# A hybrid attention, recurrence and mixture-of-experts layer: rows of most experts summed during the last five blocks, a written order of experts, and the shared expert's first products moved forward

## The chip, the cores and the metric

The kernel runs on one core of a Trainium2 chip. The metric is the device time of one execution in microseconds (us). Engines: PE (TensorE) multiplies matrices, DVE (VectorE), ACT (ScalarE) and POOL (GpSimd) work element by element, SP issues most DMAs. Each engine runs its own queue in order; semaphores join them.

## The reference

One layer over 512 latent tokens and 256 context tokens, width 1024, all float32. The first half (modulated norm, latent attention, a recurrent block, an output projection added to `x`) is not touched in what it computes. The second half is a mixture of 64 experts and one shared expert, each token using the 8 experts with the best scores:

```python
def swiglu(u, w_gate, w_up, w_down):
    return (jax.nn.silu(u @ w_gate) * (u @ w_up)) @ w_down

def moe_ffn(h, ...):                       # h: 512 x 1024
    scores = jax.nn.sigmoid(h @ router_w)  # 64 experts, groups of 8
    ...                                    # 4 best groups, then 8 best experts
    w = ROUTED_SCALE * w / w.sum(-1, keepdims=True)
    routed = routed_experts(h, eidx, w, exp_w_gate, exp_w_up, exp_w_down)
    return routed + swiglu(h, sh_w_gate, sh_w_up, sh_w_down)
```

Gate and up weights of an expert are 1024 x 256 each, its down weight 256 x 1024: 3 MiB an expert, 192 MiB for all. The result is gated, added to the residual, and normalised once more.

## The kernel before

**Stages.** By the trace's time: the modulation, input projection, recurrence and attention (to about 333 us), the output projection and the second norm (to about 390), the router and the shared expert (to 439), the 64 experts (439 to 1043), the final sum and norm (to 1113).

**Blocks of experts.** The router ranks the experts by load. Rank r has room for `caps[r]` rows, a multiple of 32; the rooms, laid end to end in the order `order`, are cut into 46 blocks of up to 128 rows. `n` is a place in that order, and a block holds rows of one to four experts. For a block, POOL gathers the tokens' rows from `h2d` (`stage_gather`, three blocks ahead), PE transposes them (`stage_trans`), multiplies by the gate and up weights (`stage_gu`, tile `gu`), transposes the product (`stage_at`) and multiplies by the down weight (`stage_down`, tile `dn`). DVE scales the result into `y`, and POOL scatters its rows to `yd` in DRAM, where each token has eight rows, one for each of its choices. PE's instructions stand in the order in which the program writes them (`manual_schedule`); the other compute engines are ordered by a scheduler with priorities.

**Weights.** There are six places for gate and up weights (tags `g0` to `g5`) and six for down weights (`d0` to `d5`). Expert `n` uses the places of `n % 6`, so its load waits until expert `n - 6` has been used for the last time. SP issues the loads in order, 1 MiB each, with at most three outstanding (`wload`). Three experts of fixed number come first; the others wait for the router's `eids`.

**The shared expert.** `sgu(t)` makes gate and up products of 128 tokens (tile `psg`), `smul` their product, `sdn` the down product and the sum with the residual `x1`, stored to `acc` in DRAM. They stand between the router's steps. The shared weights and `x1` lie in places of the experts' weights (`g4`, `d4`, `g2`).

**The end.** After the last block SP loads `acc` into `xs`. A loop over overfull experts follows (`n_ov` runs, none with these inputs), and all engines meet at it. Then SP loads the 16 MiB of `yd` in 16 pieces (`yload`, tiles `yl`), PE sums four of the eight rows of each token (`fsum`, tile `fs`), DVE adds the others, and for each 128 tokens a norm (`fsq`, `frs`) and a scaling (`fout`) lead to the store of the output.

Of the kernel before, what the change touches and what calls it, by code (L numbers as in the profile page):

```python
# [8 lines left out]
F32 = mybir.dt.float32  # L9
# [68 lines left out]
NTAIL = 8  # L78
OUTST = 3
LEAD = 22  # L80
# [20 lines left out]
def tile_kernel(tc, x, c, ctx, c_ctx, w_mod, b_mod, norm_mix_g, w_in, q_norm_g, w_q_up, kv_norm_g, w_kv_up,  # L101
# [13 lines left out]
    acc = dram.tile([S, D], F32, name="acc")  # L115
# [820 lines left out]
    x1 = pW1.tile([P, NT, D], F32, tag="g2", name="x1")  # L936
# [24 lines left out]
    wgu_s = pW1.tile([P, 2, KT, FF], F32, tag="g4", name="wgu_s")  # L961
# [21 lines left out]
    POOL.tensor_scalar(isf, ir[:, 0:E], float(NF), None, op0=OP.is_ge)  # L983
    icf = pR.tile([P, 1], F32, name="icf")
# [74 lines left out]
    @prio("sgu")  # L1059
    def sgu(t):  # L1060
        p = sgp[t] = psx("psg")
        for k in range(KT):
            PE.matmul(p, h2T[:, k, t * P:(t + 1) * P], wgu_s[:, :, k, :], start=(k == 0), stop=(k == KT - 1))
        sga[t] = et("act", "sg")
        ACT.activation(sga[t], p[:, 0:FF], AF.Silu)
# [5 lines left out]
    @prio("sdn")  # L1071
    def sdn(t):
# [3 lines left out]
        sgT = et("aT", "sgT").rearrange("p (k t) -> p k t", k=2)  # L1076
        cp("sgT", "A", sgT, pt[:, 0:FF].rearrange("p (k t) -> p k t", k=2))
        p = pw("psd")
        for n in range(2):
            for k in range(2):  # L1080
                PE.matmul(p[:, n * 512:(n + 1) * 512], sgT[:, k, :], wd_s[:, k, n * 512:(n + 1) * 512],
                          start=(k == 0), stop=(k == 1))
        tb = et("y", "tb")
        DVE.tensor_tensor(tb, p, g2b, op=OP.mult)  # L1084
        DVE.tensor_tensor(tb, tb, x1[:, t], op=OP.add)
        ACT.dma_start(acc[t * P:(t + 1) * P, :], tb)
# [38 lines left out]
    for n, r in enumerate(order):  # L1125
        for u in range(0, caps[r], 32):
            if at % P == 0:
                b = Blk()
                b.q, b.units, b.dyn = len(blocks), [], None
                blocks.append(b)  # L1130
            blocks[-1].units.append((n, r, u))
            at += 32
    for b in blocks:
        ns = [u[0] for u in b.units]
        w = 128 if len(set(ns)) == 1 else 64 if len(ns) == 4 and ns[0] == ns[1] and ns[2] == ns[3] else 32
        b.tiles = [(c, min(w, 32 * len(ns) - c)) + b.units[c // 32] for c in range(0, 32 * len(ns), w)]
        b.rows = 32 * len(ns)

        b.runs = []
        for c, (n, r, u) in enumerate(b.units):  # L1140
            if b.runs and b.runs[-1][2] == n:
                b.runs[-1][1] += 32
            else:
                b.runs.append([32 * c, 32, n, r, u])
    loads, seen, last = [], set(), {}
    for b in blocks:
        new = [n for n in dict.fromkeys(u[0] for u in b.units) if n not in seen]
        seen.update(new)
        loads += [(n, "g") for n in new] + [(n, "d") for n in new]
        for u in b.units:  # L1150
            last[u[0]] = b.q
# [3 lines left out]
    def load_upto(m):  # L1155

        while loads:
            n, what = loads[0]
            r = order[n]
            if n > m or r < E - NF and "routed" not in state or n >= NW and last[n - NW] > state["done"]:  # L1160
                return
            loads.pop(0)
            if n not in eid:
                eid[n] = r - (E - NF) if r >= E - NF else SP.value_load(eids[0:1, r:r + 1], min_val=0, max_val=E - 1)
            if what == "g":
                wg[n] = load_gu(eid[n], GS[n % NW])
            else:
                wd_[n] = load_d(eid[n], n % NW)
# [13 lines left out]
    logits(2)  # L1182
    sgu(0)
# [87 lines left out]

    for src in (pm1, ws):
# [3 lines left out]
        sT = et("sv", "sT")  # L1276
        cp("sT", "A", sT[0:E, :], p[0:E, :])
# [34 lines left out]
    def stage_gather(b, p=None):  # L1312
# [15 lines left out]
        DVE.scalar_tensor_tensor(t2[0:m], tk[0:m], float(TOPK), p[0:m, 3:4], op0=OP.mult, op1=OP.add)  # L1328
        DVE.tensor_scalar(b.iy[0:m], t2[0:m], float(FAR * TOPK), None, op0=OP.add)
# [7 lines left out]
    smul(1)  # L1337
    stage_sel(blocks[0])
    stage_sel(blocks[1])
    sdn(0)  # L1340
    sgu(2)
    stage_gather(blocks[0], pn("ix0"))
    smul(2)
    sdn(1)
    stage_gather(blocks[1], pn("ix1"))
    stage_sel(blocks[2])
    sgu(3)
    load_upto(NW - 2)
# [10 lines left out]
    st_E2 = ExitStack()  # L1359
    pE2 = st_E2.enter_context(tc.tile_pool(name="pE2", bufs=1))  # L1360
# [36 lines left out]
    def stage_down(b):  # L1397
# [8 lines left out]
        DVE.scalar_tensor_tensor(y[0:m], p[0:m], b.w[0:m], g2b[0:m], op0=OP.mult, op1=OP.mult)  # L1406
        ins = POOL.indirect_dma_start(out=yd, out_offset=bass.IndirectOffsetOnAxis(ap=b.iy[0:m, :1], axis=0),  # L1407
                                      in_=y[0:m], in_offset=None, bounds_check=S * TOPK - 1, oob_is_err=False).ins
        if b.dyn is None:
            if yw:  # L1410
                tc.declare_no_dep(ins, group="yd", reason="every token and choice has a row of its own")
            tc.add_to_no_dep_group("yd", ins)
            yw.append(ins)
# [48 lines left out]
    st_M = ExitStack()  # L1462
    st_M.enter_context(tc.manual_schedule(engines={mybir.EngineType.PE}))
# [3 lines left out]
    for i, b in enumerate(blocks):  # L1467
# [10 lines left out]
        load_upto(E - 1)  # L1478
        if i in (10, 12, 14, 16):
            got = next(table)  # L1480
            nov, ovr, obase = got or (None,) * 3
    st_M.close()

    xs = pW1.tile([P, NT, D], F32, tag=f"g{GS[(E - 6) % NW]}", name="xs")
    for t in range(NT):
        SP.dma_start(xs[:, t], acc[t * P:(t + 1) * P, :])
# [3 lines left out]
    with tc.For_i(0, n_ov, 1) as iv:  # L1490
# [3 lines left out]
        b.rows, b.q, b.tiles, b.runs = P, 0, [(0, P, -1, 0, 0)], [(0, P, -1, 0, 0)]  # L1494
# [18 lines left out]
    st_F = ExitStack()  # L1513
    psf = st_F.enter_context(tc.tile_pool(name="psf", bufs=1, space=PSUM))

# [7 lines left out]
    ydv = yd.rearrange("(t p k) f -> t p k f", p=P, k=TOPK)  # L1523
    yl = {}

    place = [GS[n % NW] for n in range(E - 5, E)]
    small = [n % NW for n in range(E - 6, E)]

    def yload(t, k0, n, buf):
        kind, i = buf  # L1530
        if kind == "g":
            z = (pW0 if i < 2 else pW1 if i < 5 else pW2).tile([P, 4, D], F32, tag=f"g{i}", name="yl")
        else:
            z = (pE2 if i == 5 else pW1).tile([P, 2, D], F32, tag=f"d{i}", name="yl")
        for k in range(0, n, 2):
            ins = SP.dma_start(z[:, k:k + 2, :], ydv[t, :, k0 + k:k0 + k + 2, :]).ins  # L1536
            for w in yw:
                after(ins, w, "rows of all experts")
            for j in range(2):
                yl[t, k0 + k + j] = z[:, k + j, :]  # L1540


    @prio("fsum")
    def fsum(t):
        p = psf.tile([P, D], F32, tag="fs", name="fs", bufs=2)
        for n0 in range(0, D, 512):
            for k in range(4):
                PE.matmul(p[:, n0:n0 + 512], ident, yl[t, k][:, n0:n0 + 512], start=(k == 0), stop=(k == 3))  # L1548
        for k in range(4, TOPK):
            DVE.tensor_tensor(xs[:, t], xs[:, t], yl[t, k], op=OP.add)  # L1550
        DVE.tensor_tensor(xs[:, t], xs[:, t], p, op=OP.add)  # L1551
# [26 lines left out]
    for t in range(NT):  # L1578
        if t < 2:
            yload(t, 0, 4, ("g", place[2 * t]))  # L1580
            yload(t, 4, 4, ("g", place[2 * t + 1]))
        elif t == 2:
            yload(t, 0, 4, ("g", place[4]))
            yload(t, 4, 2, ("d", small[0]))
            yload(t, 6, 2, ("d", small[1]))
        else:
            for k in range(0, TOPK, 2):
                yload(t, k, 2, ("d", small[2 + k // 2]))
    for t in range(NT):
        fsum(t)  # L1590
        fsq(t)
        frs(t)
        fout(t)
    st_F.close()
# [32 lines left out]
```

## Time and profile before

| | us |
|---|---|
| median of 3 runs | 1115.37 (1114.18 to 1116.23) |
| the profiled execution | 1114.81 |
| its span, first to last instruction | 1112.8 |
| outside the span | 2.0 |
| PE busy | 996.2 (90% of the span) |
| DVE, ACT, POOL busy | 484.3, 255.7, 223.4 |

The span is what the rows below are measured in: a time in them is counted from the span's start. A busy PE does not say that PE works at its peak, and its clock has two levels: PEclk is the share that was granted. An engine's row names the line of the kernel, the operation, what it writes and reads, and in brackets the idle time before it with what ended it. A DMA row (SPq) is the issue, not the transfer.

### The profile page before, as it was taken

Reading aid. Unit: us, or ns where it says so; the run is one execution under the profiler, and the core shown is the slowest. Engines: PE = TensorE matmul, PEld = TensorE weight load, DVE = VectorE, ACT = ScalarE, POOL = GpSimd, SP = SyncE. Lnnn points to the kernel's source line nnn. Section 1 sums busy time; section 2 is a strip of 40 time slices with the busy share of each in tenths; the row PEclk is TensorE's granted clock in tenths of the full one; section 3 lists DMA queues with packets and bytes.
Section 4 is the critical chain, followed back from the end, with each engine's and each line's share of the span. In section 5 each row is a group of like instructions: output and inputs, shape, how many; then the busy total and the mean of one; then the engine's idle time right before and its main releaser. Section 6 shows DMA issues by size and latency. Waiting matters only on the chain. (4 is left out here: it accounts for less than half of the span.)

```text
span 1112.8 us, 17435 instructions
## 1 busy us (share of the span) xinstructions
PE 996.2 (90%) x6813; PEld 515.6 (46%) x6813; DVE 484.3 (44%) x1064; ACT 255.7 (23%) x468; POOL 223.4 (20%) x219
## 2 busy tenths in 40 slices
PE   3899989799989998999999999999999999995482
PEld 2687654567779853443443344333333333331131
DVE  5527594988765865223222232222322223220065
ACT  3433545756661210011000110000100001000011
POOL 3382341346100001111111111111111111110001
PEclk9899999889999999999999999999999999997797
DMA  9834644200009543999999898989879999989694
GB/s 294 266 96 154 206 161 133 77 1 1 1 2 365 226 195 132 416 394 417 419 409 360 333 390 346 395 323 399 339 289 401 399 413 414 399 319 414 251 421 186
DMA packets 75404, 310.34 MB, mean 279 GB/s; under 512 B 12747, under 2 KB 31234, under 8 KB 48442
## 3 DMA queue, kind: packets, MB, share of 16 engines
q1 hardware_dynamic: 60412, 271.79, 63.2%
q0 software_dynamic: 13936, 34.26, 8.1%
q10 hardware_dynamic: 974, 3.17, 0.8%
q8 instruction: 54, 0.88, 0.3%
q14 instruction: 28, 0.23, 0.1%
HBM read 293.31 MB, written 30.29 MB: 291 GB/s over the span
## 5 line engine op out<-in xcount | busy, mean ns | idle before, releaser
L1382 PE MATMUL gu<-wgu,hT 128*32 128x512 f32 (+2 forms) x2160 | 333.0, 597 | 11.1 <-DMA wgu<-in_exp_w_up_dram 10.4
L1382 PEld LDWEIGHTS gu<-wgu,hT 128*32 128x32 f32 (+2 forms) x2160 | 105.4, 120 | 230.2 <-issue 225.9
L1403 PE MATMUL dn<-wd,aT 128*32 128x512 f32 (+2 forms) x1080 | 169.1, 596 | 16.6 <-ACT aT L124 15.4
L1385 DVE TENSOR_TENSOR act<-act,gu 128x256 f32<-128x256 f32 (+1 forms) x46 | 19.4, 421 | 297.8 <-ACT act L1384 297.8
L1384 ACT ACTIVATE act<-gu 128x256 f32<-128x256 f32 (+1 forms) x46 | 17.7, 385 | 511.7 <-PE gu L1382 511.7
L1332 POOL DMA_INDIRECT hg<-h2d,bix x46 | 47.6, 1034 | 425.9 <-issue 310.4
L1406 DVE SCALAR_TENSOR_TENSOR y<-dn,bw,g2b 128x1024 f32<-128x1024 f32 (+1 forms) x46 | 59.0, 1283 | 138.2 <-PE dn L1403 138.2
L1403 PEld LDWEIGHTS dn<-wd,aT 128*32 128x32 f32 (+2 forms) x1080 | 48.7, 119 | 100.8 <-issue 78.8
L1407 POOL DMA_INDIRECT yd<-y,biy x46 | 46.8, 1017 | 191.9 <-DVE y L1406 182.5
L1370 PEld LDWEIGHTS tr<-ident,hg 128*128 128x128 f32 (+1 forms) x368 | 39.9, 141 | 37.1 <-issue 34.1
L1370 PE MATMUL tr<-ident,hg 128*128 128x128 f32 (+1 forms) x368 | 49.7, 278 | 1.3 <-DVE tb L1084 1.3
L1548 PE MATMUL fs<-yl,ident 128*128 128x512 f32 x64 | 32.1, 654 | 20.3 <-DMA yl<-yd 18.1
L829 PE MATMUL pTr<-ident,P 128*128 128x128 f32 x192 | 30.7, 300 | 9.8 <-DVE P L820 7.7
L1306 DVE TENSOR_TENSOR sv<-iot,posR 128x256 bf16<-128x256 f32 (+3 forms) x93 | 37.1, 411 | 0.0
L812 DVE TENSOR_REDUCE nm<-pS 128x1 f32<-128x768 f32 x32 | 30.3, 951 | 11.2 <-PE pS L810 10.8
L124 ACT COPY PT<-pTr 128x384 f32<-128x384 f32 x64 | 28.0, 482 | 29.0 <-PE pTr L829 28.7
L124 ACT COPY hT<-tr 128x512 f32<-128x512 f32 (+1 forms) x46 | 26.9, 584 | 34.0 <-PE tr L1370 32.5
L840 PE MATMUL po<-PT,vsb 128*64 128x128 f32 x384 | 30.8, 299 | 1.7 <-ACT PT L124 1.7
L454 PE MATMUL pmx<-wm,csil 128*32 128x512 f32 x128 | 31.9, 606 | 0.0
L124 DVE COPY hT<-tr 128x512 f32<-128x512 f32 (+1 forms) x46 | 31.3, 680 | 0.0
L1548 PEld LDWEIGHTS fs<-yl,ident 128*128 128x128 f32 x64 | 12.7, 208 | 39.8 <-DMA yl<-yd 20.4
L829 PEld LDWEIGHTS pTr<-ident,P 128*128 128x128 f32 x192 | 24.1, 153 | 14.8 <-issue 7.7
(473 smaller groups left out, 1472.9 us busy)
## 6 DMA issues: line engine op xcount, KB each, us to landing
wgu<-in_exp_w_gate_dram SPq DMA_DIRECT2D x64, 1024.0 KB
wgu<-in_exp_w_up_dram SPq DMA_DIRECT2D x64, 1024.0 KB
wd<-in_exp_w_down_dram SPq DMA_DIRECT2D x64, 1024.0 KB
wm<-in_w_mod_dram SPq DMA_DIRECT2D x32, 512.0 KB
yl<-yd SPq DMA_DIRECT2D x16, 1024.0 KB
wm<-in_w_mod_dram SPq DMA_DIRECT2D x8, 1024.0 KB
win<-in_w_in_dram SPq DMA_DIRECT2D x5, 1024.0 KB
xz<-in_x_dram SPq DMA_DIRECT2D x4, 512.0 KB
```

The lines of the kernel that those rows point to most:

```text
L124: (e.copy if e is ACT else e.tensor_copy)(dst, src)
L454: PE.matmul(pm[32 * g:32 * g + 32, :], csil[:, kk, :], wmp[n, g // 2][:, (g % 2) * 512:(g % 2 + 1) * 512], start=(kk == 0), stop=(kk == KT ...
L829: PE.transpose(p[:, j * P:(j + 1) * P], Pm[u][:, k * P:(k + 1) * P], ident)
L840: PE.matmul(po[i][64 * hh:64 * hh + 64, t * P:(t + 1) * P], vsb[:, k, 2 * i + hh, :], PTt[i, t, hh][:, k, :], start=(k == 0), stop=(k == N ...
L1306: DVE.tensor_tensor(sv[:, :, c:c + w], iot[:, u:u + w][:, None, :].to_broadcast([P, NT, w]), col_[:, :, None].to_broadcast([P, NT, w]), op ...
L1332: POOL.indirect_dma_start(out=b.hg[0:m], out_offset=None, in_=h2d, in_offset=bass.IndirectOffsetOnAxis(ap=b.ix[0:m, :1], axis=0), bounds_c ...
L1370: PE.transpose(p[:, i * m:(i + 1) * m], b.hg[0:m, (i0 + i) * P:(i0 + i + 1) * P], ident[0:m, 0:m])
L1382: PE.matmul(p[c:c + w, :], b.hT[:, k, c:c + w], wg[n][:, :, k, :], start=(k == 0), stop=(k == KT - 1))
L1403: PE.matmul(p[c:c + w, n0:n0 + 512], b.aT[:, k, c:c + w], wd_[n][:, k, n0:n0 + 512], start=(k == 0), stop=(k == 1))
L1406: DVE.scalar_tensor_tensor(y[0:m], p[0:m], b.w[0:m], g2b[0:m], op0=OP.mult, op1=OP.mult)
L1407: ins = POOL.indirect_dma_start(out=yd, out_offset=bass.IndirectOffsetOnAxis(ap=b.iy[0:m, :1], axis=0), in_=y[0:m], in_offset=None, bounds ...
L1548: PE.matmul(p[:, n0:n0 + 512], ident, yl[t, k][:, n0:n0 + 512], start=(k == 0), stop=(k == 3))
```

## The change

In the diff's order. (1) The experts' order is written out. The last five ranks in it have room for at most 128 rows, and each starts a block of its own (`LATE = 5`); there are still 46 blocks. (2) The rows of these five blocks are no longer scattered to `yd`: POOL adds them by an accumulating DMA to `acc`, which has 128 rows more for empty places. (3) Since their rows of `yd` are not written now, `yd` is filled with zeros from `zt` during the attention: 16 MiB in four DMAs and 0.5 MiB for the new rows of `acc`. (4) `sgu` is written further forward, the third tile in three pieces between the router's steps; the down products are split in two halves on other PSUM tiles; the residual is kept in place (`x1`). `x1` and the shared gate and up weights change places (`g2`, `g4`), and `d4` and `d5` do. The places of `d5` are opened earlier, and so is the load of experts 3 and 4 (`load_upto(NW - 2)`). (5) `sum_loads` issues the 16 loads of `yd` after the blocks 40 to 45, each pair of rows to a place of weights that has been used for the last time. The sums in PE and DVE stand before the loop over overfull experts, the first adds before the last block. (6) DVE's order is the written one from the first block on. (7) At the end `acc` is loaded as `ya`, and one add for each 128 tokens joins it to the sum.

```diff
+ORDER = [61, 62, 63, 35, 60, 48, 52, 21, 43, 38, 9, 50, 34, 2, 46, 28,
...
+LATE = 5
+    acc = dram.tile([S + P, D], F32, name="acc")
+    zt = modrow.rearrange("p a b -> p (a b)")
+    POOL.memset(zt, 0.0)
+    SP.dma_start(acc[S:S + P, :], zt)
+    for t in range(NT):
+        SP.dma_start(yd.rearrange("(t p k) f -> t p k f", p=P, k=TOPK)[t], zt[:, None, :].to_broadcast([P, TOPK, D]))
...
-    x1 = pW1.tile([P, NT, D], F32, tag="g2", name="x1")
+    x1 = pW1.tile([P, NT, D], F32, tag="g4", name="x1")
-    wgu_s = pW1.tile([P, 2, KT, FF], F32, tag="g4", name="wgu_s")
+    wgu_s = pW1.tile([P, 2, KT, FF], F32, tag="g2", name="wgu_s")
...
+    def sdp(t):
+        tb = et("y", "tb")
+        x_ = x1[:, t]
+        for n0 in range(0, D, 512):
+            p = psx("psd")
             for k in range(2):
+                PE.matmul(p, sgT[t][:, k, :], wd_s[:, k, n0:n0 + 512], start=(k == 0), stop=(k == 1))
+            DVE.tensor_tensor(tb[:, n0:n0 + 512], p, g2b[:, n0:n0 + 512], op=OP.mult)
+        DVE.tensor_tensor(x_, tb, x_, op=OP.add)
+        ACT.dma_start(acc[t * P:(t + 1) * P, :], x_)
...
+    GS, DS, NW = (5, 0, 1, 2, 3, 4), (0, 1, 2, 3, 5, 4), 6
...
+        if n >= E - LATE:
+            at = 0
...
+        if b.late:
+            DVE.tensor_scalar(b.iy[0:m], tk[0:m], float(FAR), spad[0:m], op0=OP.add, op1=OP.min)
...
+        if b.late:
+            POOL.indirect_dma_start(out=acc, out_offset=bass.IndirectOffsetOnAxis(ap=b.iy[0:m, :1], axis=0),
+                                    in_=y[0:m], in_offset=None, bounds_check=S + P - 1, oob_is_err=True, compute_op=OP.add)
+            return
...
+    pairs = [(t, k) for t in range(NT) for k in range(0, TOPK, 2)]
+    homes = [("d", E - 6)] + [(w, n) for n in range(E - 5, E) for w in "dgh"]
+    def sum_loads(i):
...
+        while rest and last[rest[0][1][1]] <= i:
+            (t, k), (w, n) = rest.pop(0)
...
+            ins = SP.dma_start(z, ydv[t, :, k:k + 2, :]).ins
...
+        if not loads:
+            sum_loads(i)
+        if i == NB - 2:
+            for k in (0, 2, 4):
+                add_pair(0, k, k == 0)
...
+    add_pair(0, 6, False)
+    for t in range(1, NT):
...
+        for k in range(4):
+            for h in range(2):
+                PE.matmul(fs[h], ident, yl[t, k - k % 2][:, k % 2, h * 512:(h + 1) * 512], start=(k == 0), stop=(k == 3))
+        add_pair(t, 4, True)
+        add_pair(t, 6, False)
+        for h in range(2):
+            x_ = xs[:, t, h * 512:(h + 1) * 512]
+            DVE.tensor_tensor(x_, x_, fs[h], op=OP.add)
...
-    for t in range(NT):
-        SP.dma_start(xs[:, t], acc[t * P:(t + 1) * P, :])
...
+    for t in range(NT):
+        SP.dma_start(ya[:, t], acc[t * P:(t + 1) * P, :])
     def fsum(t):
...
+        DVE.tensor_tensor(xs[:, t], xs[:, t], ya[:, t], op=OP.add)
```

How it moves instructions at the end, on SP. Before, from the last expert's load to the loop over overfull experts (L1489 and L1490):

```order
L1104 ISA
L1104 DMA wd<-in_exp_w_down_dram 128x2048
L1486 DMA xs<-acc 128x1024 x4
L1489 TENSOR_LOAD nov
L1489 ISA x2
L1490 COMPARE_AND_BRANCH
L1490 UNCONDITIONAL_BRANCH x2
```

The 16 loads of `yd` (L1536) stand behind that loop there. Now, on SP, the same stretch (the loop is L1578 and L1579):

```order
L1119 ISA
L1119 DMA wd<-in_exp_w_down_dram 128x2048
L1523 DMA yl<-yd 128x2048 x16
L1578 TENSOR_LOAD nov
L1578 ISA x2
L1579 COMPARE_AND_BRANCH
L1579 UNCONDITIONAL_BRANCH x2
```

The 16 loads have moved ahead of the loop, and the load of `acc` behind it.

On PE, the last two blocks before (`gu` gate and up products, `tr` and `at` transposes, `dn` down products; 32 rows of an expert to a matmul):

```order
L1403 MATMUL dn<-wd,aT 32x512 x16
L1382 MATMUL gu<-wgu,hT 32x512 x32
L1370 MATMUL tr<-ident,hg 128x96 x8
L1393 MATMUL at<-ident,act 128x128 x2
L1403 MATMUL dn<-wd,aT 32x512 x16
L1382 MATMUL gu<-wgu,hT 32x512 x24
L1393 MATMUL at<-ident,act 128x96 x2
L1403 MATMUL dn<-wd,aT 32x512 x12
L1489 TENSOR_LOAD nov
```

These two blocks hold seven experts. PE's last two blocks now, and what follows them:

```order
L1438 MATMUL dn<-wd,aT 128x512 x4
L1417 MATMUL gu<-wgu,hT 128x512 x8
L1405 MATMUL tr<-ident,hg 128x128 x8
L1428 MATMUL at<-ident,act 128x128 x2
L1438 MATMUL dn<-wd,aT 128x512 x4
L1417 MATMUL gu<-wgu,hT 128x512 x8
L1428 MATMUL at<-ident,act 128x128 x2
L1438 MATMUL dn<-wd,aT 128x512 x4
L1569 MATMUL fs<-yl,ident 128x512 x24
L1578 TENSOR_LOAD nov
```

Each block is one expert now, and 24 of the 32 matmuls of the sum stand before the loop, right behind the last down product.

## Rows read from the trace of the kernel before

**Rows 1.** The page's first line.
```profile
span 1112.8 us, 17435 instructions
```
**Rows 2.** Stretches: length, busy time of PE, PEld, DVE, ACT, POOL; PEclk, DMA share, GB/s.
```profile
700.00:800.00 100.00, 97.29 (x942) 35.10 (x942) 27.61 (x81) 9.96 (x24) 16.22 (x16) 1.00 0.93 367
...
1000.00:1050.00 50.00, 29.30 (x174) 8.19 (x174) 4.25 (x6) 1.94 (x5) 2.91 (x3) 0.82 0.82 333
```
**Rows 3.** Timeline of PE: start, length, instruction; blocks 0, 2, 43, 44 and 45.
```profile
441.04 8.82 PE L1382 MATMUL gu<-wgu,hT 128*128 128x512 f32 x16 [0.77 <-DVE hT L124]
...
467.76 7.03 PE L1382 MATMUL gu<-wgu,hT 128*128 128x512 f32 x16
...
986.30 7.05 PE L1382 MATMUL gu<-wgu,hT 128*32 128x512 f32 x64
...
998.83 1.03 PE L1382 MATMUL gu<-wgu,hT 128*32 128x512 f32 x6
...
1012.01 3.62 PE L1403 MATMUL dn<-wd,aT 128*32 128x512 f32 x26 [1.14 <-DMA wd<-in_exp_w_down_dram]
1017.97 1.89 PE L1382 MATMUL gu<-wgu,hT 128*32 128x512 f32 x2 [2.34 <-DMA wgu<-in_exp_w_up_dram]
...
1028.78 8.40 PE L1382 MATMUL gu<-wgu,hT 128*32 128x512 f32 x44 [3.64 <-DMA wgu<-in_exp_w_up_dram]
...
1039.04 3.63 PE L1403 MATMUL dn<-wd,aT 128*32 128x512 f32 x24 [0.46 <-ACT aT L124]
```
**Rows 4.** Timeline of SP's issues in the experts' stage.
```profile
449.00 2.80 SPq L1104 DMA_DIRECT2D wd<-in_exp_w_down_dram  x2
...
580.85 2.99 SPq L1104 DMA_DIRECT2D wd<-in_exp_w_down_dram  x2
...
993.36 0.34 SPq L1104 DMA_DIRECT2D wgu<-in_exp_w_gate_dram  x1
...
1023.14 5.96 SPq L1104 DMA_DIRECT2D wd<-in_exp_w_down_dram  x3
```
**Rows 5.** Waits of SP's queue: in total, times, longest.
```profile
SPq L1104 <- PE gu L1382: 93.6, 18, 10.9
...
SPq L1104 <- DVE tb L1085: 32.1, 1, 32.1
```
**Rows 6.** Timeline around the end of the last block and the final sum, several engines.
```profile
1042.74 1.28 DVE L1406 SCALAR_TENSOR_TENSOR y<-dn,bw,g2b 96x1024 f32<-96x1024 f32 x1 [4.69 <-PE dn L1403]
1044.29 0.95 POOL L1407 DMA_INDIRECT yd<-y,biy  x1 [26.09 <-DVE y L1406]
1049.20 0.34 SPq L1518 DMA_DIRECT2D fgb<-in_final_norm_g_dram  x1
1049.59 26.75 SPq L1536 DMA_DIRECT2D yl<-yd  x16
...
1056.10 11.96 PE L1548 MATMUL fs<-yl,ident 128*128 128x512 f32 x20 [13.42 <-DMA yl<-yd]
...
1079.62 5.42 PE L1548 MATMUL fs<-yl,ident 128*128 128x512 f32 x12 [1.53 <-DMA yl<-yd]
```
**Rows 7.** The chain that ended last: start, length, piece.
```profile
1033.75 14.53 another core or an unknown queue
...
1097.68 1.23 DVE xs L1551
...
1102.99 1.15 ACT xs L1573
```
**Rows 8.** Timeline of SP and DVE: loads of 0.5 MiB on idle queues.
```profile
196.84 1.91 SPq L784 DMA_DIRECT2D wor<-in_w_out_dram  x2
332.84 0.34 SPq L943 DMA_DIRECT2D g1b<-mrd  x1
...
340.06 0.42 DVE L1007 TENSOR_TENSOR x<-x,tm 128x256 f32<-128x256 f32 x1 [1.81 <-DMA x<-in_x_dram]
```
**Rows 9.** Timeline of PE: the first transpose of block 0.
```profile
439.18 1.09 PE L1370 MATMUL tr<-ident,hg 128*128 128x128 f32 x8 [1.32 <-DVE tb L1084]
```

More of the change, by code (lines that the diff above doesn't have):

```diff
@@ L983, in tile_kernel @@
     POOL.tensor_scalar(isf, ir[:, 0:E], float(NF), None, op0=OP.is_ge)
+    spad = pR.tile([P, 1], F32, name="spad")
+    POOL.tensor_scalar(spad, ic, float(S), None, op0=OP.add)
     icf = pR.tile([P, 1], F32, name="icf")
@@ L1144, in tile_kernel @@
                 b.runs.append([32 * c, 32, n, r, u])
+    for b in blocks[-LATE:]:
+        b.late = True
     loads, seen, last = [], set(), {}
@@ L1148, in tile_kernel @@
         seen.update(new)
-        loads += [(n, "g") for n in new] + [(n, "d") for n in new]
+        loads += [(n, w) for n in new for w in ("dg" if n == NF else "gd")]
         for u in b.units:
@@ L1461, in tile_kernel, with add_pair @@
     load_upto(NW - 1)
-    st_M = ExitStack()
-    st_M.enter_context(tc.manual_schedule(engines={mybir.EngineType.PE}))
+    st_M.enter_context(tc.manual_schedule(engines={mybir.EngineType.DVE}))
+    ydv = yd.rearrange("(t p k) f -> t p k f", p=P, k=TOPK)
+    pairs = [(t, k) for t in range(NT) for k in range(0, TOPK, 2)]
+    homes = [("d", E - 6)] + [(w, n) for n in range(E - 5, E) for w in "dgh"]
+    yl, rest, place = {}, list(zip(pairs, homes)), {}
+    xs = None
+    def sum_loads(i):
+        nonlocal xs
+        if xs is None and i >= last[E - 6]:
+            xs = pW1.tile([P, NT, D], F32, tag=f"g{GS[(E - 6) % NW]}", name="xs")
+        while rest and last[rest[0][1][1]] <= i:
+            (t, k), (w, n) = rest.pop(0)
+            g, d = GS[n % NW], DS[n % NW]
+            if w == "d":
+                z = (pE2 if d == 5 else pW1).tile([P, 2, D], F32, tag=f"d{d}", name="yl")
+            else:
+                if w == "g":
+                    place[n] = (pW0 if g < 2 else pW1 if g < 5 else pW2).tile([P, 4, D], F32, tag=f"g{g}", name="yl")
+                z = place[n][:, 0:2, :] if w == "g" else place[n][:, 2:4, :]
+            ins = SP.dma_start(z, ydv[t, :, k:k + 2, :]).ins
+            for y_ in yw:
+                after(ins, y_, "rows of all blocks but the last")
+            yl[t, k] = z
+    def add_pair(t, k, first):
+        x_ = xs[:, t]
+        for j in range(2):
+            if first and j == 0:
+                DVE.tensor_tensor(x_, yl[t, k][:, 0, :], yl[t, k][:, 1, :], op=OP.add)
+            elif not first:
+                DVE.tensor_tensor(x_, x_, yl[t, k][:, j, :], op=OP.add)
     stage_trans(blocks[0])
@@ L1493, in tile_kernel @@
         b = Blk()
-        b.rows, b.q, b.tiles, b.runs = P, 0, [(0, P, -1, 0, 0)], [(0, P, -1, 0, 0)]
+        b.rows, b.q, b.tiles, b.runs, b.late = P, 0, [(0, P, -1, 0, 0)], [(0, P, -1, 0, 0)], True
         wdma.clear()
@@ L1521, in tile_kernel @@
     fe = [pick("fx0", "D"), pick("fx1", "P"), pick("fx2", "D"), pick("fx3", "D")]
[L1523 to L1540, printed above, removed]
+    n = E - 5
+    ya = (pW0 if GS[n % NW] < 2 else pW1 if GS[n % NW] < 5 else pW2).tile([P, NT, D], F32, tag=f"g{GS[n % NW]}", name="ya")
+    for t in range(NT):
+        SP.dma_start(ya[:, t], acc[t * P:(t + 1) * P, :])
     @prio("fsum")
     def fsum(t):
[L1545 to L1551, printed above, removed]
+        DVE.tensor_tensor(xs[:, t], xs[:, t], ya[:, t], op=OP.add)
     @prio("fsq")
@@ L1578, in tile_kernel @@
     for t in range(NT):
[L1579 to L1589, printed above, removed]
         fsum(t)
```

113 lines of the change are left out of this document (56 added, 57 removed), and 3 rows, old and new, of the table ORDER.

## The prediction

> **What bounds the kernel now.** I read the stretches first, then PE's timeline, then SP's, then the chain. In the middle of the experts' stage PE is busy for 97.29 of 100 us at the full clock, the DMA engines for 0.93 of the time [rows 2]: the two are nearly balanced, and the reader must see which waits for which. PE's timeline says it: from block 0's first product at 441.04 to block 44's at 998.83 the 44 blocks take 557.8 us, 12.7 each, whatever their mixture of experts; a block's gate and up products take 7.03 with one expert and 7.05 with four matmuls side by side [rows 3]. SP waits for PE to free places (93.6 us in 18 waits, rows 5), not PE for SP. So PE bounds 44 blocks. At the end that turns round. Blocks 44 and 45 hold seven experts, and their places come free late: at 993.36 SP issues a load just as block 43's products end (986.30 + 7.05 = 993.35), and the last three loads stand at 1023.14 [rows 3, 4]. PE waits in block 44 and four times in block 45, whose down product ends at 1039.04 + 3.63 = 1042.67. In the stretch 1000 to 1050 the granted clock is 0.82 on average [rows 2].
>
> Behind it comes a tail of 1112.8 - 1042.7 = 70.1 us [rows 1, 3] in which DMA sets the pace: SP has been at the loop since 1033.75 and leaves it when the last scatter is down, at 1048.28; the loads of the rows are issued from 1049.59 and PE sums them as they land from 1056.10 [rows 6, 7].
>
> **The change part by part.** I call T the end of the last block's down product, and compare with the span of 1112.8.
>
> *Blocks.* 46 blocks as before, and the columns that PE streams in one don't depend on its experts (above), so 46 at the same pace, if the weights are there. Blocks 44 and 45 now take 43.9 us (998.83 to 1042.67) in place of two at 12.55 (pitch of blocks 42 to 43: 998.83 - 986.30 = 12.53), that is 25.1. Gain: 18.7. Do the weights come? While loads are dense, 45 issues pass from 449.00 to 580.85, 2.93 us each, 8.8 an expert [rows 4]. The written order needs experts 3 to 24 for block 15, which starts at 441 + 15 x 12.65 = 631: 22 x 8.8 = 194 us of loading, begun at 440 as before, ends at 634, begun at about 421, when the shared products leave their place, at 615. The earlier start is there: SP waited 32.1 us for the residual's place [rows 5], which now belongs to expert 5. Later the demand falls: up to block 39, 55 experts need 484 us and have 511. The last three experts' loads can go when block 39 is done, and the first is wanted at block 43, three blocks or 38 us later, for 26 us of loads. So I take all 18.7; its bounds are 0 and 18.7.
>
> *Start of block 0.* The shared expert's and the router's products are the same ones in another order. PE waited just 1.32 us before block 0's first transpose, for the last down product's eviction [rows 9]; that wait stays. In the written order PE may wait for the router's selection where it used to fill in products. I take 0, bounds -4 (no wait, no slow first product: 8.82 against 7.03, rows 3) and +4.
>
> *Zeros.* SP's queue is empty from 198.75 (196.84 + 1.91) to 332.84 [rows 8], 134 us; 16.5 MiB are 17.3 MB, at the 367 GB/s of rows 2 some 47 us. Behind the four DMAs in SP's queue stands only the load of 332.84. POOL's fill of 1024 columns has no row; it is hidden unless it delays POOL's rotary work behind it. 0, bounds -2 and +3 (DVE's and PE's order in the attention also shifts a little, and some twenty small DVE instructions of the overfull table leave it).
>
> *The late adds.* Five accumulating DMAs in place of five scatters. The last scatter was down 4.0 us after its issue (1044.29 to 1048.28, rows 6, 7). No row shows an accumulating one. It must be down before the loop's meeting point, some 23 us after its issue. I take it as hidden; bounds 0 and the rival below.
>
> *DVE's five adds before the last block's product.* 5 x 1.23 (the add in rows 7) = 6.2 us behind `y` of block 44, beside 7.05 us of products of block 45: hidden if rows 0 to 5 of the first tokens have landed; their loads are issued after blocks 40 and 41. In the sum 0, bounds 0 and +1.
>
> *The tail.* From T: `y` 1.35 (1042.74 + 1.28 - 1042.67), for the sum's first tile takes `dn`'s place. Then 24 matmuls; the trace shows each as two passes, 48 in all. At the full clock 12 take 5.42, so 0.43 each when loads don't hold them up [rows 6]: 20.6. Their data is there: the last three loads go out at T and land by T + 10, while the third tile begins at T + 15. DVE's adds of SBUF rows lie beside PE; behind its last matmul come two half adds, 1.3. Then the meeting point: from there to the next load 0.9 at least (1048.28 to 1049.20), at most the 5.2 from `y`'s end at 1044.02 to 1049.20; I take 2.0, since no scatter is left to wait for. So the load of the last norm's gain (`fgb`) is issued at T + 25.3, where before it was at T + 6.5.
>
> Behind it 4 loads of 0.5 MiB in place of 16 MiB. The nearest rows are a broadcast row and the first 0.5 MiB behind it: 332.84 to 340.06, 7.2 us [rows 8]. The four tiles then go through add, square, root and scaling. One alone takes 1104.14 - 1097.68 = 6.5 from the add to the end of scaling [rows 7]. For the three others DVE adds 1.23 for the sum and about 1.4 for root and scaling each: 6.5 + 3 x 2.6 = 14.4. From there to the span's end it is 1112.8 - 1104.14 = 8.7 as now. Tail: 25.3 + 7.2 + 14.4 + 8.7 = 55.6, against 70.1: 14.5 less. Bounds: 48 us (root and scaling of early tiles beside late loads, 1 us at the loop) and 79.
>
> The upper bound is the clock. After an idle time of 2.34 us two matmuls took 1.89 us; after one of 1.14, 26 went through in 3.62, the full rate [rows 3]. The wait for `y` is 1.35 plus hand-over, between the two. The first 20 matmuls of the sum at 1056.10, after 13.4 us of idleness, took 11.96. At half clock 48 cost 41 us.
>
> TensorE: Matmul & The Clock Gate, in the Trainium skill, says under "HAM oscillation — how this bites in real kernels" that a PE which waits between bursts falls to 1.2 GHz and starts the next burst there; rows 3 agree at 2.34 us. By that rule the sums would begin slow; by the row of 1.14 they don't. This is the second rival.
>
> *Sum.* -18.7 + 0 + 0 - 14.5 = -33.2. Against the profiled execution, 1114.81, this gives 1081.6. That one lay 0.6 below the median of the three, so I forecast 1082.
>
> **Rivals.** (a) *The weights stay late.* The bytes to load do not change, and the DMA engines are 0.93 busy: blocks with many new experts now stand earlier, and the wait of 18.7 may go there instead of vanishing. For it: at 2.93 us a load, block 15 would have 16 us of margin or, without the earlier start, -3. Against it: 93.6 us of waits for places. Time: 1082 + 18.7 = 1101; some of it is likelier than all.
>
> (b) *The sums run at the low clock*, as said: +20.3, 1102; if only the first third does, 1089. For it rows 3 at 2.34, against it the row at 1.14 and that PE has been busy without a break for 46 blocks.
>
> (c) *The accumulating DMAs are slow, and the kernel is slower than before.* Each add waits for the one before, since all write `acc`. The first is issued near T - 48 (four blocks and `y`), so the fifth is down at T - 48 + 5d. It shows from T + 24, d = 14.4, and eats the whole gain of 33 at d = 21; beyond that each us of d costs 5. At d = 25 the time is 1082 + 5 x 25 - 72 = 1135. Against it: a scatter took 4.0, so d would be over five times as much.
>
> DMA: Bandwidth & Descriptors, in the Trainium skill, says among its rules for kernel authors that an accumulating DMA reads its destination and writes it later. By that, an estimate of twice the bytes of a scatter, d would be about 8, and hidden; no run here shows it yet.
>
> (d) *The overlap does not come about.* If the loads of `yd` are held on SP until the last block (each needs a freed place and every earlier scatter), only the wait of blocks 44 and 45 goes and PE sums behind the loads as before: 1114.8 - 18.7 = 1096. Against it: the scatter of block 39 is five blocks old by then, and three loads, 9 us, go out per block of 12.6.
>
> **How the numbers follow.** Forecast 0.70, own range 1072 to 1091. (a) 0.09, (b) 0.08, (c) 0.03, (d) 0.04, and 0.06 for a shorter tail and start near 1068. Leaving out the lower half of that last case, (c), and the upper parts of (a) and (b) is 0.15: range 1069 to 1099. A measurement tells 0.2%, 2.2 us, from no change. All cases but (c) are faster: 0.95; same 0.02; slower 0.03.
>
> **What would show it.** Right: PE without a wait over 1 us on weights from block 0 to 45, T near 1022, the `yl` loads issued between the blocks 40 and 45, the 48 passes of the sum in about 21 us, the loads of `ya` 25 to 28 us behind T. Wrong: waits of PE for `wgu` in the blocks 12 to 20, passes of 0.85 us, a meeting point that ends with a POOL transfer, or block 0 later than 445.

## The result, and the profile after

The changed kernel takes 1076.2 us (median of 4 runs, 1075.4 to 1081.0) against 1115.8 of the kernel before on the same chip: a ratio of 0.965, 95% interval 0.962 to 0.969. The forecast was 1082, with a range of 1069 to 1099. The page's first line, for [rows 1]:

```profile
span 1073.6 us, 16081 instructions
```

So 39.2 us of span are gone. T, the end of the last down product, is the place to cut them. PE's timeline for blocks 0, 44 and 45 and the sums (start, length, instruction, idle time before it), for [rows 3, 6, 9]:

```profile
440.08 7.13 PE L1417 MATMUL gu<-wgu,hT 128*128 128x512 f32 x16 [0.77 <-DVE hT L130]
...
997.31 7.03 PE L1417 MATMUL gu<-wgu,hT 128*128 128x512 f32 x16
...
1018.89 3.70 PE L1438 MATMUL dn<-wd,aT 128*128 128x512 f32 x8 [0.52 <-ACT aT L130]
1023.97 20.87 PE L1569 MATMUL fs<-yl,ident 128*128 128x512 f32 x48 [1.38 <-DVE y L1441]
```

T is 1018.89 + 3.70 = 1022.6, where it was 1042.7. From block 0's first product to T it is 582.5 us instead of 601.6; from T to the span's end 51.0 instead of 70.1. Each part gives 19.1, the earlier start of block 0 gives 1.0. No block waits for weights any more (the longest such wait left is some 0.2 us, at block 17), and the 48 passes run at 0.43 us each.

The middle stretch, for [rows 2] (length; busy time of PE, PEld, DVE, ACT, POOL; PEclk, DMA share, GB/s):

```profile
700.00:800.00 100.00, 96.96 (x761) 36.85 (x758) 28.61 (x80) 10.03 (x24) 16.70 (x16) 1.00 1.00 400
```

PE is as busy as before in the middle, but the DMA engines went from 0.93 to 1.00: nothing is left over there. SP's timeline and then its waits (total, times, longest), for [rows 4, 5]:

```profile
409.62 0.37 SPq L1119 DMA_DIRECT2D wd<-in_exp_w_down_dram  x1
422.01 0.33 SPq L1119 DMA_DIRECT2D wgu<-in_exp_w_gate_dram  x1
...
431.48 0.33 SPq L1119 DMA_DIRECT2D wd<-in_exp_w_down_dram  x1
447.02 0.34 SPq L1119 DMA_DIRECT2D wgu<-in_exp_w_gate_dram  x1
...
984.17 0.33 SPq L1119 DMA_DIRECT2D wd<-in_exp_w_down_dram  x1
984.68 39.21 SPq L1523 DMA_DIRECT2D yl<-yd  x16
1047.96 0.34 SPq L1604 DMA_DIRECT2D fgb<-in_final_norm_g_dram  x1
1048.35 2.04 SPq L1612 DMA_DIRECT2D ya<-acc  x4
```

```profile
SPq L1119 <- DMA wd<-in_exp_w_down_dram: 148.9, 59, 4.2
...
SPq L1119 <- DMA acc<-x: 10.7, 2, 6.4
...
SPq L1119 <- PE gu L1417: 7.8, 5, 5.2
```

The waits for PE's products, 93.6 us in [rows 5], are down to 7.8; SP waits for its own loads in flight. It did that before too, a line of that view that [rows 5] doesn't have:

```profile
SPq L1104 <- DMA wd<-in_exp_w_down_dram: 122.8, 53, 4.3
```

With the waits for gate and up loads it was 337 us before and is 405 now: the loads were near their limit already. The loads of rows start right behind the last load of weights, at the end of block 42 and not of block 40, and 13 of the 16 are out before T. The tail, for [rows 6, 7]:

```profile
1042.63 2.48 DVE L1534 TENSOR_TENSOR xs<-xs,yl 128x1024 f32<-128x1024 f32 x2 [1.33 <-DMA yl<-yd]
1045.22 1.28 DVE L1574 TENSOR_TENSOR xs<-xs,fs 128x512 f32<-128x512 f32 x2
...
1053.62 2.48 DVE L1616 TENSOR_TENSOR xs<-xs,ya 128x1024 f32<-128x1024 f32 x2 [7.12 <-DMA ya<-acc]
...
1059.62 4.57 DVE L1640 SCALAR_TENSOR_TENSOR xs<-xs,rf,fgb 128x1024 f32<-128x1024 f32 x2
...
1060.02 6.36 POOL L1637 TENSOR_TENSOR xs<-xs,fgb 128x1024 f32<-128x1024 f32 x2 [32.25 <-ACT jk L1620]
...
1066.88 2.19 ACT L1638 ACTIVATE xs<-xs,rf 128x1024 f32<-128x1024 f32 x2 [2.30 <-DVE rf L1631]
```

The reader sees four pieces: sums to 1046.5, a meeting point to 1047.96, a residual load to 1053.62, the norm to 1069.07, and behind them 4.5 us to the span's end.

### The profile page after: what moved, and what is told of

The parts are those of the page before. It is cut to its first block, busy times and chain, and to the rows that moved or that the text cites. A ratio compares the mean times of both kernels' runs of the same rounds, so it can differ in the third digit from the quotient of the medians.

```text
span 1073.6 us, 16081 instructions
## 1 busy us (share of the span) xinstructions
PE 974.9 (91%) x6125; PEld 521.9 (49%) x6125; DVE 494.6 (46%) x1062; ACT 255.4 (24%) x468; POOL 232.0 (22%) x221
## 5 line engine op out<-in xcount | busy, mean ns | idle before, releaser
L1417 PE MATMUL gu<-wgu,hT 128*32 128x512 f32 (+3 forms) x1776 | 325.6, 594 | 0.8 <-DVE hT L130 0.8
L1417 PEld LDWEIGHTS gu<-wgu,hT 128*32 128x32 f32 (+3 forms) x1776 | 111.9, 127 | 206.8 <-issue 203.4
L1438 PE MATMUL dn<-wd,aT 128*32 128x512 f32 (+3 forms) x888 | 168.5, 597 | 16.3 <-ACT aT L130 16.3
L1420 DVE TENSOR_TENSOR act<-act,gu 128x256 f32<-128x256 f32 (+1 forms) x46 | 19.4, 421 | 270.2 <-ACT act L1419 270.2
L1365 POOL DMA_INDIRECT hg<-h2d,bix x46 | 50.3, 1094 | 415.0 <-issue 309.9
L1438 PEld LDWEIGHTS dn<-wd,aT 128*32 128x32 f32 (+3 forms) x888 | 52.1, 127 | 97.0 <-issue 76.2
L1446 POOL DMA_INDIRECT yd<-y,biy x41 | 41.2, 1004 | 138.6 <-DVE y L1441 125.3
L1335 DVE TENSOR_TENSOR sv<-iot,posR 128x256 bf16<-128x256 f32 (+3 forms) x86 | 34.0, 435 | 0.0
L826 ACT ACTIVATE P<-pS,nm 128x768 f32<-128x768 f32 x32 | 29.0, 908 | 7.0 <-DVE nm L824 6.9
L1078 PE MATMUL psg<-wgu_s,h2T 128*128 128x512 f32 x64 | 29.0, 598 | 0.0
```

What stands on the lines that cost most here:

```text
L1335: DVE.tensor_tensor(sv[:, :, c:c + w], iot[:, u:u + w][:, None, :].to_broadcast([P, NT, w]), col_[:, :, None].to_broadcast([P, NT, w]), op ...
L1365: POOL.indirect_dma_start(out=b.hg[0:m], out_offset=None, in_=h2d, in_offset=bass.IndirectOffsetOnAxis(ap=b.ix[0:m, :1], axis=0), bounds_c ...
L1417: PE.matmul(p[c:c + w, :], b.hT[:, k, c:c + w], wg[n][:, :, k, :], start=(k == 0), stop=(k == KT - 1))
L1438: PE.matmul(p[c:c + w, n0:n0 + 512], b.aT[:, k, c:c + w], wd_[n][:, k, n0:n0 + 512], start=(k == 0), stop=(k == 1))
```

## Experiments

Medians (4 to 10 runs) and ratios are measured times; each ratio is to runs of the kernel before on the same chip, one of two. The last two columns cut the profiled execution of each, in us, at block 0's first product and T:

| kernel | median | ratio to before (95%) | block 0 to T | T to end |
|---|---|---|---|---|
| before | 1115.8 | | 601.6 | 70.1 |
| changed | 1076.2 | 0.965 (0.962 to 0.969) | 582.5 | 51.0 |
| order alone | 1108.1 | 0.993 (0.991 to 0.996) | 593.9 | 70.4 |
| early start alone | 1114.1 | 0.9985 (0.9975 to 0.9995) | 601.3 | 70.2 |
| changed, no early start | 1088.2 | 0.974 (0.972 to 0.976) | 594.4 | 52.6 |
| changed, loads written last | 1077.5 | 0.965 (0.963 to 0.967) | 582.9 | 52.7 |
| changed, no overlap | 1104.1 | 0.989 (0.987 to 0.991) | 585.9 | 77.7 |
| changed, zeros twice | 1074.6 | 0.963 (0.961 to 0.966) | 582.9 | 51.9 |
| changed, late rows not added | 1080.0 | 0.967 (0.965 to 0.969) | 586.5 | 53.8 |
| changed, loop first | 1088.7 | 0.976 (0.973 to 0.978) | 585.5 | 59.3 |
| changed, other norm | 1072.4 | 0.960 (0.958 to 0.962) | 582.5 | 47.4 |
| the same, residual loaded early | 1068.2 | 0.957 (0.955 to 0.959) | 583.3 | 45.5 |
| the same, gate and up places first | 1069.3 | 0.957 (0.956 to 0.959) | 583.1 | 44.9 |

**The order alone.**

```diff
-    order = [E - NF + j for j in range(NF)]
...
+    order = ORDER
```

> The kernel before with the list ORDER alone: no late blocks, no earlier loads, the sums where they were. Theory (the order ends the waits of blocks 44 and 45, and the tail stays as it was): 18.7 us less than before, 1097 us, with a tail of 70 us from the end of the last down product. Rival (the order only works with the earlier start of the loads: in the changed kernel the loads for blocks 13, 15, 17, 36 and 39 arrived with 2 us or less to spare, and the first routed load was issued 8.5 us earlier than before, at 440.5 instead of 449.0): the tensor engine waits up to 7 us for weights in blocks 13 to 17, and the time is about 1104 us. Second rival (the order matters little, the gain is all in the tail): 1115 us.

1108.1: between the first theory and the second rival, 4 us above the first rival. The waits at the end are gone, but new ones of PE stand at blocks 13 and 40:

```profile
610.97 8.66 PE L1376 MATMUL gu<-wgu,hT 128*32 128x512 f32 x58 [4.11 <-DMA wgu<-in_exp_w_up_dram]
...
958.71 8.72 PE L1376 MATMUL gu<-wgu,hT 128*32 128x512 f32 x58 [2.14 <-DMA wgu<-in_exp_w_up_dram]
```

The first puts all later blocks 6.8 us behind the changed kernel's, the second 4.9 more. Only 7.7 us of the stage are won. The second has a cause of its own: without `LATE` the last experts are cut on from block to block, so block 40 holds rows of experts 58 and 59 and wants 59 a block earlier.

**The early start taken out of the changed kernel.**

```diff
-    x1 = pW1.tile([P, NT, D], F32, tag="g4", name="x1")
+    x1 = pW1.tile([P, NT, D], F32, tag="g2", name="x1")
...
-        loads += [(n, w) for n in new for w in ("dg" if n == NF else "gd")]
+        loads += [(n, w) for n in new for w in "gd"]
...
-    load_upto(NW - 2)
     smul(2)
...
+    load_upto(NW - 2)
     sdt(2)
```

> The changed kernel with the earlier start of the loads undone (x1 and the shared weights in their old places, the sixth place for down weights opened after the shared expert, the third routed group asked for where it was asked for before). Theory (thin margins of 2 us or less at blocks 13 to 17, and DMA engines that are busy all the time from 500 to 1000 us): the first routed load comes some 8 us later, the tensor engine waits about 7 us in blocks 13 to 17, and the time is about 1083 us. Rival (the loads catch up, the margins are wide enough, as the prediction said of block 15): 1076 us, no difference. Second rival (the late loads push the last weight load and the first loads of rows back as well): up to 1090 us.

1088.2, 12 us slower: the first theory, with a larger size. (The second rival's part is small at most: the tail is 1.6 us longer.) My 8.5 us of head start was read off wrongly: SP's first routed gate load is issued at 442.18 here and at 422.01 in the changed kernel, 20 us apart.

```profile
442.18 0.37 SPq L1119 DMA_DIRECT2D wgu<-in_exp_w_gate_dram  x1
```

PE's timeline has the waits from block 8 on, the largest at blocks 12 and 13:

```profile
595.84 7.03 PE L1417 MATMUL gu<-wgu,hT 128*32 128x512 f32 x58 [1.94 <-DMA wgu<-in_exp_w_up_dram]
...
612.81 7.03 PE L1417 MATMUL gu<-wgu,hT 128*32 128x512 f32 x58 [3.09 <-DMA wgu<-in_exp_w_up_dram]
```

By block 18 this kernel is 11.2 us behind, at T 11.9. Of the stage 7.2 us are won, about as with the order alone.

**The early start alone.** The same edits as above, the other way round, in the kernel before (with `sgu` forward and a block's loads expert by expert, as in the change).

> The kernel before with the earlier start of the loads alone (x1 and the shared weights in exchanged places, gate and up products of the shared expert first, the sixth place for down weights opened early), with its own order of experts and its own tail. Theory (order and early start are worth something only together: the order alone gave 7.7 us of the experts' stage and the early start added 11.8 to it; with the old order the places, not the loads, set the pace up to block 43, so a head start is lost there, and blocks 44 and 45 wait as before): experts' stage some 600 us as before, 1114 to 1116 us in all, perhaps 1 to 2 us less at block 0. Rival (the two add up): the head start of some 10 us carries through to blocks 44 and 45, 1104 us.

1114.1: the theory. The routed gate loads start at 424.01, 2 us behind the changed kernel's, but that buys 0.3 us of the stage, since PE waits at the end as it always did:

```profile
424.01 0.34 SPq L1113 DMA_DIRECT2D wgu<-in_exp_w_gate_dram  x1
```

```profile
1004.02 9.64 PE L1401 MATMUL gu<-wgu,hT 128*32 128x512 f32 x58 [4.84 <-DMA wgu<-in_exp_w_up_dram]
...
1028.58 9.32 PE L1401 MATMUL gu<-wgu,hT 128*32 128x512 f32 x44 [7.47 <-SPq L1507]
```

So of 19.1 us in the stage the order gives 7 to 8 (7.7 alone, 7.2 with the late blocks' own cut), the early start alone 0.3, and the rest, over 11, comes only from both together. Block 0's first product runs at the full clock in all of these (7.13 us for 8.82), so 1.7 of the order's 7 to 8 is not the order's. What the five blocks of their own and DVE's written order give by themselves was not measured.

**The overlap, twice.** First the loads were only written behind the last block:

```diff
-        if not loads:
+        if i == NB - 1:
             sum_loads(i)
-        if i == NB - 2:
```

> The changed kernel with all sixteen loads of rows issued after the last block, as the kernel before had them, and everything else kept. Theory (the tail is shorter because the loads lie under the last five blocks): the first sum starts about 6.5 us after the last down product, as it did before, and lasts 29 us to its last pass with the loads setting the pace; then 2 us, 5.7 us for the first tile of the residual, 15.4 and 4.5 us as now: a tail of 65 us instead of 51.0, and 1090 us (the prediction's rival d said 1096). Rival (the loads hide anyway behind the tensor engine's 48 passes, and the gain of the tail came from the tiles of the residual being loaded once): 1076 to 1080 us.

1077.5, no difference, and no test of the overlap: the scheduler, which orders SP's queue, moved the loads forward again. At T only the last three go out, as in the changed kernel:

```profile
1024.18 1.27 SPq L1523 DMA_DIRECT2D yl<-yd  x3
```

It shows one thing: all of DVE's adds of rows stand behind the last `y` here, and the last sum ends 25.6 us behind T for 23.9. So the five adds that the change puts before it buy at most 1.7 us, which the medians (1077.5 and 1076.2) can't tell from nothing. Then each load was made to wait for the last `y`:

```diff
+            after(ins, blocks[-1].yi, "not before the last block")
```

> The changed kernel with each of the sixteen loads of rows made to wait for the last block's own result, so that none can be issued before it (in the run before this one the scheduler had moved the issues back under the last blocks, so it undid nothing). Theory (the overlap is what shortens the tail): the last pass of the sums ends 35.5 us after the first issue, as in the kernel before (1049.59 to 1085.04), so some 37 us after the last down product instead of 22.2; 15 us more, 1091 us. Rival (16.8 MB hide behind 48 passes of 0.43 us, and the tail is shorter for another reason): below 1080 us.

1104.1, nearly 28 us slower, 26.7 of it in the tail. The overlap is what shortens it, at almost twice the price expected. SP's loads, PE's sums and DVE's last add of rows:

```profile
1027.57 25.30 SPq L1523 DMA_DIRECT2D yl<-yd  x16
```

```profile
1045.19 8.76 PE L1569 MATMUL fs<-yl,ident 128*128 128x512 f32 x16 [18.97 <-DVE xs L1535]
1055.08 7.13 PE L1569 MATMUL fs<-yl,ident 128*128 128x512 f32 x16 [1.13 <-SPq L1579]
1065.05 8.83 PE L1569 MATMUL fs<-yl,ident 128*128 128x512 f32 x16 [2.84 <-DMA yl<-yd]
```

```profile
1072.57 2.49 DVE L1535 TENSOR_TENSOR xs<-xs,yl 128x1024 f32<-128x1024 f32 x2 [1.33 <-DMA yl<-yd]
```

From the first issue to DVE's last add of rows, which waits for its load, it is 45 us for 16.8 MB, and PE sums only what has landed. In the kernel before it is much the same: the DMA engines are full from the first issue at 1049.59 to 1096 (0.99 in the last 4 us). The 35.5 us of the expectation end at a pass that was not PE's last. The tail is even 7.6 us longer than before's. There each tile's norm lay beside the next tile's loads, and the residual was loaded ahead of the meeting point: 5.2 us from the last sum to the last scaling. Here all of that stands behind the last sum and takes 22.9.

**Zeros twice.** `for t in [*range(NT), *range(NT)]` around the fill.

> The changed kernel with the zeros of yd written twice, 17 MB more by four more DMAs issued at 199 us. Theory (nothing on that queue is due before 332 us): no difference, 1076 us. Rival (the extra writes take DMA time from the loads of the stage between 200 and 330 us): the four writes landed 23.6 us after issue, so a second set costs up to 24 us, 1100 us.

1074.6: nothing. (Two of the four executions are 4 to 6 us shorter than the other two; the profiled one is the shortest, and its block 0 starts at 435.10, 5.0 us earlier than the changed kernel's. Why is not shown.) The DMA share from 200 to 300 us goes from 0.47 in the changed kernel to 0.87 here, and PE is no less busy:

```profile
200.00:300.00 100.00, 85.55 (x590) 67.61 (x591) 84.87 (x121) 63.51 (x132) 43.51 (x42) 0.91 0.47 187
```

```profile
200.00:300.00 100.00, 87.82 (x633) 69.53 (x632) 84.61 (x126) 66.03 (x138) 36.71 (x22) 0.93 0.87 352
```

**Late rows not added.** `compute_op=OP.add` left out.

> The changed kernel in which the last five blocks write their rows over the residual's instead of adding to them (so the sum of those rows is left out). Theory (the five adding transfers are hidden: four lie under blocks, the fifth has 20 us until the residual is read): 1074 to 1078 us, no difference. Rival (an adding transfer is slow enough to hold the meeting point or the residual's load): 1 to 6 us less, and an earlier first residual tile.

1080.0, but not for that reason: the stage is 4.0 us longer in this execution, by small waits for weights at blocks 15, 17, 36 and 39. From T the first residual tile comes at 30.7 us, in the changed kernel at 31.0. So the adding costs at most 0.3. The time from issue to landing here (the last number; of the five the trace times only the last):

```profile
acc<-y,biy POOLq DMA_INDIRECT x5, 9.3
```

**A faster norm.** The load of `fgb` right behind the last block, and the scalings `fx2` and `fx3` on DVE too.

> The changed kernel with the final norm's weight row loaded right after the last block instead of behind the meeting point, and all four tiles scaled on VectorE (GpSimd and ScalarE out of it). Theory (the row's load holds up the residual tiles behind it, and the two scalings of 2.28 us beside GpSimd's products take 1.28 us without them): first residual tile 1 to 2 us earlier, adds to last scaling about 12 us instead of 15.4: 4 to 5 us less, 1071 us. Rival (VectorE becomes the bound, four scalings of 1.28 us behind each other, and the row's load costs nothing): 1075 to 1077 us.

1072.4, as the theory said. SP and DVE:

```profile
1049.90 1.75 SPq L1612 DMA_DIRECT2D ya<-acc  x4
```

```profile
1053.11 2.56 DVE L1616 TENSOR_TENSOR xs<-xs,ya 128x1024 f32<-128x1024 f32 x2 [4.65 <-DMA ya<-acc]
...
1060.23 2.48 DVE L1640 SCALAR_TENSOR_TENSOR xs<-xs,rf,fgb 128x1024 f32<-128x1024 f32 x2
```

The first residual tile comes 3.2 us behind its issue, where it took 5.3 when the row's load stood just before it; a scaling takes 1.24 instead of 2.28.

**The loop ahead of the sums.**

```diff
     add_pair(0, 6, False)
-    for t in range(1, NT):
...
     st_M.close()
...
+    st_M.enter_context(tc.manual_schedule(engines={mybir.EngineType.PE, mybir.EngineType.DVE}))
+    fsum(0)
+    fsq(0)
+    for t in range(1, NT):
...
         fsum(t)
+        frs(t - 1)
+        fout(t - 1)
```

The sums now stand behind the loop, each tile is finished beside the next one's sum, and all four scalings are on DVE.

> The changed kernel with the overflow loop moved ahead of the sums of tiles 1 to 3, so that the residual tiles and the norm's row load while TensorE adds rows, each tile finished as soon as its sum is there, and all four scalings on VectorE. Theory (meeting point, residual load and the first tiles' ends are hidden by the 48 passes): sums from about 4 to 25 us after the last down product, then one tile's end of about 8 us and 4.5 us to the span's end: a tail of 38 us instead of 51.0, 1063 us. Rival (TensorE, having waited 4 us at the meeting point, runs the sums at the lower clock, as the first product after a wait of 2.34 us took 8.82 instead of 7.13 us in the kernel before; or the last three row loads share the DMA engines with the residual tiles): sums end at 30 to 45 us, 1068 to 1080 us.

1088.7: 12 us slower, and for a reason that I did not have. SP, the chain that ended last, then PE:

```profile
1027.76 1.27 SPq L1523 DMA_DIRECT2D yl<-yd  x3
1045.60 0.34 SPq L1589 DMA_DIRECT2D fgb<-in_final_norm_g_dram  x1
```

```profile
1028.60 16.33 DMA yl<-yd
...
1044.95 0.03 SPq L1565
```

```profile
1046.32 22.44 PE L1640 MATMUL fs<-yl,ident 128*128 128x512 f32 x48 [18.59 <-issue]
```

The engines leave the meeting point (L1565) 18 us after T, when the last load of rows is down: SP goes on at once behind it. PE, which could have summed the rows that were there, stood still. The slower clock that the rival feared cost 22.44 - 20.87 = 1.6. (The 8.82 us that the rival quotes are block 0's, after waits of 1.32 and 0.77; after 2.34 two matmuls took 1.89.)

**The residual loaded early** (on top of the faster norm).

```diff
     SP.dma_start(fgb, final_norm_g[None, :].to_broadcast([P, D]))
+    ya = (...).tile([P, NT, D], F32, ..., name="ya")
+    for t in range(NT):
+        SP.dma_start(ya[:, t], acc[t * P:(t + 1) * P, :])
     for t in range(1, NT):
```

> The kernel of the run e3_tail in which the residual tiles are also loaded right behind the last rows, ahead of the meeting point (and again inside the overflow loop, should that run). Theory (after the meeting point the tail waits only for that load: 4.7 us idle on VectorE in that run): the load lies beside the sums, the first add starts right behind the meeting point, 3 to 5 us less than e3_tail, 1068 us. Rival (the DMA engines are the bound of the sums: the last rows land some 20 us after issue, and 2 MB more behind them land 5 us later, so the meeting point moves by as much): 1072 us, no gain.

1068.2, the lowest median of all. Its tail is 1.9 us shorter than the faster norm's in the traces; the medians say 4 us, but they come from two chips, and the single runs overlap (1066.8 to 1071.4 and 1068.9 to 1073.0). The trace stands between theory and rival:

```profile
1036.80 2.16 SPq L1566 DMA_DIRECT2D ya<-acc  x4
```

```profile
yl<-yd SPq DMA_DIRECT2D x16, 1024.0 KB, 20.9
...
ya<-acc SPq DMA_DIRECT2D x4, 512.0 KB, 13.3
...
acc<-y,biy POOLq DMA_INDIRECT x5, 10.6
```

The fifth add holds the loads on SP until 1036.8, and from there they take 13.3 us beside the last rows (median from issue to landing), so the residual comes no sooner than 28.8 us behind T (1052.96), where it came at 30.0 with the faster norm.

**The gate and up places first**: `"ghd"` for `"dgh"` in `homes`.

> The kernel of e10_ya in which each of the last five experts' places takes its three pairs in the order gate, up, down: the gate and up places are free 5.7 us before the down place, and the down pair no longer holds the other two back on SyncE. Theory (rows are issued late): two of the last three loads are issued some 5 us earlier and land earlier, VectorE does not wait for tile 3's rows, 0 to 2 us less than e10_ya. Rival (the loads stand in line in the DMA engines, not at SyncE): no difference.

1069.3, the rival: two of the last three loads are issued 5.3 to 5.7 us before T, where all three went out at T, and DVE starts on their rows only half a us earlier (18.9 us behind T for 19.4). The line is in the DMA engines.

## Why the prediction was right, and where it was not

*Blocks, -18.7.* Blocks 44 and 45 take 25.3 us (997.31 to 1022.59) instead of 43.85: 18.6, as forecast. But the margin behind it failed: "at 615" for block 15 at 631, 16 us to spare, "-3" without the earlier start. There was next to none, and that it sufficed was luck: in kernels with the same loads this stage came out 0 to 4.0 us longer by small waits at blocks 13 to 17 and 36 to 39, perhaps a part of the spread of 1075 to 1081 too. (The three longest, 585.5 to 586.5, are from one chip, which also gave 582.5; what makes the difference is open.) Without the early start 11.9 us are lost, not 3. Three terms were mis-sized. The loads did not run from 421 without a break: six were out at 431.48, then SP stood until 447.02, 10.7 us of it for the stores of the residual (`acc<-x`), whose place is now expert 5's. The pace behind the break is 3.05 us (61 issues from 454.58 to 640.77), not 2.93. So the other 60 loads that block 15 needs are through at 447 + 60 x 3.05 = 630, just when it starts (629.68). And block 13 is as tight: it needs experts 20 and 21 at 604.0, 51 loads behind the break, at 602.6. The slack for the last three experts held. Rival (a) is thus what happens, in two thirds of its size, when the early start is missing.

*Start, 0.* Block 0's product began 1.0 us earlier and ran at the full clock, 7.13 for 8.82: -2.7, inside the bounds of 4.

*Zeros, late adds, five adds: 0 each.* Borne out by the runs above. The five adds lay beside block 45's products as said, from 1011.23 to 1017.48. The late adds were nearer to their limit than the argument said. It went by a scatter's 4.0 us; with the DMA engines full an adding DMA takes 10.6 and a plain one to the same rows 9.3, against the 14.4 at which rival (c) begins to show. The adding itself accounts for 1.3 of the 10.6, and the crowd of other transfers probably for the rest. By the Trainium skill (DMA: Bandwidth & Descriptors, Rules for kernel authors) I had estimated 8, from twice the bytes.

*Tail, 55.6.* It is 51.0. `fgb` at T + 25.4 (forecast 25.3); sums 20.9 (20.6); first residual tile 5.7 later (7.2); add to scaling 15.4 (14.4, since two scalings take 2.28 each while POOL multiplies); end 4.5 (8.7). The last, from the last scaling to the span's end, was the largest miss: I took it over from the kernel before. It is 8.7 to 8.8 in the three kernels with the old end, 3.7 to 4.5 in nine of the ten with the new one and 7.7 in the other (late rows not added); what sets it stays open. And "land by T + 10" failed: the last rows come some 20 us after T. It cost just 1.4 and 1.3 us of DVE's waits, because PE's 48 passes take as long.

*The rivals.* (b) didn't come: PE waited 1.38 us for `y` and went on at 0.43 a pass. The Trainium skill's rule on a PE that waits between bursts (TensorE: Matmul & The Clock Gate, HAM oscillation) did bite after some waits in other runs here and not after others, below. (d) was priced 14.5 and costs 28: it took the old tail as its price, and the new tail without overlap is 7.6 us longer than that.

So the time was right by 6 us with the mechanism right. By spans, 1079.6 forecast and 1073.6 measured, the 6.0 us are 2.7 at the start and 4.6 in the tail, less 1.3 that the blocks fell short. Most of the tail's 4.6 is the end, which no argument foresaw. The margin of the weights, the worst error, hardly shows in the sum, since the early start just covered it.

## What to carry to other kernels

When PE and the DMA engines are nearly balanced, a better order of loads and an earlier start can be worth little apart (7.7 and 0.3 us of the stage here) and much together (19.1): the order moves demand forward, the start pays for it. Check the tightest block, at the pace of loads that will hold then, and look for breaks in the loading. And before a meeting point of all engines is moved, ask which transfers are in flight there: here the engines left it only when the last of them was down.

## What the runs showed of the hardware

The length of PE's wait did not decide its clock. After 3.09 us at block 13 without the early start it stayed at 1.00; after 2.14 us at block 40 under the order alone it was at 0.83, so for a part of these 10 us at the lower of its two levels (PEclk is the last but two):

```profile
610.00:620.00 10.00, 7.19 (x60) 2.53 (x61) 1.40 (x9) 0.13 (x1) 1.01 (x1) 1.00 1.02 415
```

```profile
958.00:968.00 10.00, 9.29 (x64) 3.40 (x65) 0.12 (x1) 0.39 (x1) 0.41 (x1) 0.83 1.01 408
```

A slow start cost 1.6 to 1.7 us four times, 8.66 or 8.72 for 7.03 and 8.76 or 8.83 for 7.13, and 2.6 once, 9.64 for 7.03 in the early start alone. Loads of 1 MiB took 20.9 us from issue to landing (the median above) with the DMA engines full, though these moved one in 2.5 to 3 us: that is the line they stand in, and an earlier issue didn't shorten it (24.5 with the gate and up places first).
